# Expert weights in chunks of 128 rows by 1024 columns; light groups of two PSUM banks, heavy groups of four

## The chip, the cores and the metric

The kernel is one program on one core of a Trainium2 chip. The metric is the device time of one execution in microseconds (us), the median of several runs. The engines are TensorE (PE; its weight loads are shown apart as PEld), VectorE (DVE), ScalarE (ACT), GpSimd (POOL) and SyncE (SP), which issues nearly all DMAs. TensorE's clock has two levels, 1.2 and 2.4 GHz; the profile gives the granted clock as a share of the higher one.

## What is computed

Two layers of a diffusion backbone run over 256 latent and 256 context tokens with a width of 1024. Each layer is a modulated RMSNorm, a mixer (neighbourhood attention, differential attention, short convolution, output projection) and a feed-forward part. In the second layer that part is eight experts, of which each latent token takes two. This is the stage that the change touches:

```python
def swiglu(h, w1, w3, w2):
    return (jax.nn.silu(h @ w1) * (h @ w3)) @ w2

def moe_ffn(h, w_router, w1, w3, w2):
    logits = jnp.einsum('...d,de->...e', h.astype(jnp.float32), w_router.astype(jnp.float32))
    top_vals, top_idx = lax.top_k(logits, TOP_K)
    top_w = jax.nn.softmax(top_vals, axis=-1)
    gates = jnp.sum(jax.nn.one_hot(top_idx, N_EXPERTS, dtype=jnp.float32) * top_w[..., None], axis=-2).astype(h.dtype)
    y = jnp.zeros_like(h)
    for e in range(N_EXPERTS):
        y = y + gates[..., e:e + 1] * swiglu(h, w1[e], w3[e], w2[e])
    return y
```

`w1` and `w3` of an expert are 1024 x 3584, `w2` is 3584 x 1024, all float32. Here h has 256 tokens. The output is the RMSNorm of the latent stream after this.

## The kernel before

**Experts by rank.** The router's counts rank the experts. The program holds a branch for each pattern of counts; with these inputs the one that runs (`moe_main`) treats ranks 0 and 1 as heavy and ranks 7, 2, 3, 4, 5 as light, with room for 32 tokens each (64 for rank 2); one expert is not called on. A *heavy* expert multiplies all 256 tokens: every weight chunk is split into a high and a low part (`whi` by ACT, L467, and `wlo` by DVE, L469), and each product is three fast matmuls (L220 to L222): high by high, low by high, high by low. A *light* expert gathers its few tokens and makes plain float32 products (L1575) whose 32 tokens fill only 32 of PE's rows, so four products sit side by side; a *fold* (L1603) adds the four sums up and brings the columns into rows.

**Weights.** The 588 chunks of 512 KB of the seven experts stream in through a ring of 20 buffers (`raw`) and, at first, 16 more (`far`). A chunk is 256 rows by 512 columns, as two rows of 512 columns on each of 128 partitions (`load`, L1189); `weights` (L1343) hands out the next buffer of the ring and issues its DMA on SP's queue, which waits there until the buffer's last reader is done.

**Heavy experts.** `heavy` (L1504) goes through the 3584 hidden columns in groups of 3, 2 and 2 times 512. In a group it takes 512 columns at a time: four chunks of `w1` into two PSUM banks (of four, tag H), a Silu of both, four chunks of `w3` into the other two banks, then the product (DVE, L1539) and its split into `gh` and `gl`. Then come the group's rows of `w2`, first for the output's left half in two banks (two blocks of 128 tokens), then for the right half. After each half, `gated` (L1457, tile `of`) scales the two banks and `accumulate` (L1464) adds them to `xT`. `split_ahead` (L1356) asks for the split of one chunk more than is in use, so the split of the next chunk is written into ACT's and DVE's order at a point of its own. `heavy` yields after every chunk: 84 steps an expert.

**Light experts.** `light` (L1562) takes 512 columns of `w1` at a time, four chunks into one bank (of two, tag L), then the same of `w3`. At the end of each, ACT copies the bank to `s` (L1596), and the fold of it is run in the middle of a later group. `w2` is done for one half of the output after the other, and `scatter` (L1468) after each half scales it, splits it (`oh`, `ol`), and a later task multiplies by the selection matrix (L1482, L1483) and adds to `xT`. It yields after every two chunks: 42 steps an expert, two chunks or four products each.

**The order.** `mix_experts` (L1641) writes one program from both: a planner counts the estimated costs (`HEAVY` 2.85 for a heavy step, `PE_COST` for a light one) against the chunks loaded, and switches between heavy steps, one at a time, and bursts of two light steps (`BURST`). Matmuls are chained in exactly this order (`chained`, L1374). Before the branch, while routing is being finished, `first_steps` (L1328) already runs rank 7's first products from the 36 chunks that are loaded in advance.

```python
            elif burst == 0:
                k = "heavy" if surplus <= lead else "light"
                burst = BURST if k == "light" else 1
```

The rest of the functions that the change touches:

Of the kernel before, what the change touches and what calls it, by code (L numbers as in the profile page):

```python
# [23 lines left out]
KT = 8  # L24
# [5 lines left out]
RAW_M = 20  # L30
# [4 lines left out]
FAR = 16  # L35
ROT = 0
# [5 lines left out]
BURST = 2  # L42

# [84 lines left out]
def tile_hybrid_block(ctx: ExitStack, tc: tile.TileContext, x, c, cx, c_ctx, ada_w, ada_b, w_in, w_out, na_rpb,  # L128
# [1021 lines left out]
    def route_early():  # L1150
# [28 lines left out]
        mo["chunks7"], mo["early"] = heavy_chunks([7], (7,)), {}  # L1179
        ahead(mo["raw"])  # L1180

    def ahead(places):

        for raw in places:
            w, r, row0, c0 = next(mo["chunks7"])
            mo["early"][w.tensor.name, r, row0, c0] = raw
            load(w, slice(0, 1), row0, c0, raw)

    def load(w, e, row0, c0, raw):  # L1189
        sy.dma_start(out=raw, in_=w[0][e, row0:row0 + 256, c0:c0 + 512].rearrange("e (k p) n -> p (e k) n", p=128))  # L1190
# [6 lines left out]
    def route():  # L1197
# [7 lines left out]
        for n in ("h", "split", "hpool", "rawd"):  # L1205
# [4 lines left out]
            [128, 2, 512], F32, name=f"far{i}") for i in range(FAR)])  # L1210
# [117 lines left out]
    def first_steps():  # L1328

        run = mo["run7"] = light((7,), 32)  # L1330
        while mo["early"]:
            next(run)
            mo["run7_done"] = mo.get("run7_done", 0) + 1
        while mo["folds"]:
            mo["folds"].popleft()()
        mo["run7_tasks"] = list(tasks)
        tasks.clear()
        mo["far"].close()

# [3 lines left out]
    def weights(w, r, row0, c0):  # L1343

        raw = mo["early"].pop((w.tensor.name, r, row0, c0), None)
        if raw is None:
            raw = mo["ring"].popleft()
            if r < 7 and r not in mo["e"]:
                mo["e"][r] = nc.values_load(mo["ints"][0:1, 1, r:r + 1], engines=[mybir.EngineType.SP], min_val=0,
                                            max_val=NE - 1)  # L1350
            load(w, bass.ds(mo["e"][r], 1) if r < 7 else slice(0, 1), row0, c0, raw)
        if any(raw is q for q in mo["raw"]):
            mo["ring"].append(raw)
        return raw

    def split_ahead(chunks):  # L1356
# [3 lines left out]
        def make():  # L1360
            for args in chunks:
                raw = weights(*args)
                hi, lo = (mo["split"].tile([128, 2, 512], F32R, name=n, tag=n) for n in ("whi", "wlo"))
                parts(raw, hi, lo)
                yield hi, lo
        todo = make()
        ready.append(next(todo))
# [100 lines left out]
    def scatter(o, h, selT, gate, after):  # L1468

        big = mo["big"]  # L1470
        while mo["adds"]:
            mo["adds"].popleft()()
        of = gated(o, h, gate)
        oh = big.tile([128, 512], F32R, name="oh", tag="oh")
        ol = big.tile([128, 512], F32R, name="ol", tag="ol")
# [14 lines left out]
    def heavy_chunks(ranks, groups):  # L1490

        for r in ranks:
            j0 = 0
            for nj in groups:
                for j in range(j0, j0 + nj):
                    for w in (moe_w1, moe_w3):
                        for u in range(4):
                            yield w, r, u * 256, j * 512
                for h in range(2):
                    for q in range(2 * nj):  # L1500
                        yield moe_w2, r, j0 * 512 + q * 256, h * 512
                j0 += nj

    def heavy(last, ranks):  # L1504
# [3 lines left out]
        pieces = split_ahead(heavy_chunks(ranks, mo["groups"]))  # L1508
        for r in ranks:
            j0 = 0  # L1510
            for nj in mo["groups"]:
                gh, gl = (mo["gated"].tile([128, 4 * max(mo["groups"]), 256], F32R, name=n, tag=n)
                          for n in ("gh", "gl"))
                for j in range(nj):
                    sa = None
                    for w in range(2):
                        a = [pbank("H").rearrange("p (a b) -> p a b", a=2) for _ in range(2)]
                        for k in range(0, KT, 2):
                            wh, wl = next(pieces)
                            for kk in range(2):  # L1520
                                kt = k + kk
                                for f in range(4):
                                    fs = slice(f * 128, (f + 1) * 128)
                                    for q in mm3(a[f // 2][:, f % 2, :], wh[:, kk, fs], wl[:, kk, fs], xs[0][:, kt, :],
                                                 xs[1][:, kt, :], kt == 0 and f % 2 == 0, kt == KT - 1):
                                        chained(q)
                            if k < KT - 2:
                                yield
                        if sa is None:
                            sa = [xT[:, 4 * i:4 * i + 4, 384:512] for i in range(2)]  # L1530
                            a = [q.rearrange("p a (b c) -> p (a b) c", c=128) for q in a]
                            for i in range(2):
                                act.activation(sa[i], a[i], AF.Silu)
                        else:
                            for i in range(2):
                                f0 = 4 * j + 2 * i
                                q, gs = a[i].rearrange("p a (b c) -> p (a b) c", c=128), [
                                    v[:, f0:f0 + 2, :].rearrange("p a (b c) -> p (a b) c", c=128) for v in (gh, gl)]
                                dve.tensor_tensor(out=sa[i], in0=sa[i], in1=q, op=ALU.mult)  # L1539
                                parts(sa[i], *gs)  # L1540
                        yield
                j0 += nj
                for h in range(2):
                    o = [pbank("H") for _ in range(2)]
                    for f0 in range(0, 4 * nj, 2):
                        wh, wl = next(pieces)
                        for k in range(2):
                            f = f0 + k
                            for b in range(2):
                                bs = slice(b * 128, (b + 1) * 128)  # L1550
                                for q in mm3(o[b], gh[:, f, bs], gl[:, f, bs], wh[:, k, :], wl[:, k, :], f == 0,
                                             f == 4 * nj - 1):
                                    chained(q)
                        if f0 < 4 * nj - 2:
                            yield
                    for b in range(2):
                        accumulate(b, h, gated(o[b], h, mo["rk"][:, 2 + b, r:r + 1]))
                    if j0 == 7 and r == ranks[-1]:
                        last(h)
                    yield  # L1560

    def light(ranks, n, last=None):  # L1562
# [16 lines left out]
        for i, r in enumerate(ranks):  # L1579
# [4 lines left out]
            for j in range(7):  # L1584
                for w in (moe_w1, moe_w3):
                    a = pbank("L")
                    for u in range(4):
                        raw = weights(w, r, u * 256, j * 512)
                        for k in range(2):
                            product(a, x[:, 2 * u + k, i * n:(i + 1) * n], raw[:, k, :], 2 * u + k, KT)  # L1590
                        if u == 1:
                            yield
                    while folds:
                        folds.popleft()()
                    s = mo["pool"].tile([128, 512], F32, name="s", tag="s", bufs=2)
                    act.activation(s, a, AF.Copy)  # L1596

                    def fold(s=s, gs=g[j], first=w is moe_w1):

                        p = pbank("tg")[:, :4 * n].rearrange("p (a b) -> p a b", a=4)  # L1600
                        if n == 32:
                            for c in range(4):
                                chained(pe.matmul(p[32 * c:32 * c + 32], fold32,  # L1603
                                                  s.rearrange("p (q c i) -> p c q i", c=4, i=32)[:, c], start=True,
                                                  stop=True, tile_position=(0, 32 * c), skip_group_check=True))
                            t = mo["pool"].tile([128, 4, n], F32, name="sT", tag="sT", bufs=2)
                            dve.transpose(out=t, in_=p)  # L1607
                            p = t
                        else:
                            for f in range(4):  # L1610
                                chained(pe.matmul(p[:, f, :], s[:, f * 128:(f + 1) * 128], mo["fold", n], start=True,
                                                  stop=True))
                        if first:
                            act.activation(gs, p, AF.Silu)
                        else:
                            dve.tensor_tensor(out=gs, in0=gs, in1=p, op=ALU.mult)
                    folds.append(fold)
                    yield
                if j == 3:
                    tasks.append(place)  # L1620
            end = i == len(ranks) - 1
            if end:
                mo["following"]()
            for h in range(2):
                o = pbank("L")
                for q in range(14):
                    raw = weights(moe_w2, r, q * 256, h * 512)
# [211 lines left out]
```

## Time and profile before

| | us |
|---|---|
| median of 3 runs | 1720.82 |
| lowest, highest | 1720.62, 1724.28 |
| the profiled execution | 1725.1 |
| its span, first to last instruction | 1723.4 |
| PE busy | 1651.9 |
| DVE busy | 1022.4 |
| ACT busy | 633.3 |

The profile is of one execution: its own time is 1725.1 us, of which 1723.4 lie between the first and the last instruction. Busy times are of the whole span; the expert stage is the second half of it, from about 880 us on, and is read by windows. In a timeline row the bracket is the idle time before the instruction and what ended it. The mean granted clock of the span is 0.980.

### The profile page before, as it was taken

The page shows a single profiled execution, that of the slowest core. Times are in us where ns is not written, and L with a number is a line of the kernel's source. Part 1 is how long each engine was busy: PE and PEld are TensorE (multiplying, and loading weights), DVE is VectorE, ACT ScalarE, POOL GpSimd, SP SyncE. Part 2 cuts the span into 40 slices and gives each one's busy share as a digit, 9 for nine tenths or more (in the row PEclk, how much of TensorE's full clock was granted, in tenths as well). Part 3 has the DMA queues.
Part 4 walks back from the last instruction along what each step waited for, and adds up shares of the span by engine and source line. Part 5 has one row for each costly group of instructions (what it writes and reads, how often), then busy time and mean ns, then how long its engine had stood idle before and what let it go on. Part 6 is the DMA issues. An engine that isn't in the chain of part 4 may idle for free.

```text
span 1723.4 us, 28476 instructions
## 1 busy us (share of the span) xinstructions
PE 1651.9 (96%) x10942; PEld 1269.6 (74%) x10942; DVE 1022.4 (59%) x2027; ACT 633.3 (37%) x1057; POOL 17.4 (1%) x27
## 2 busy tenths in 40 slices
PE   7999999999999999999987999999999999999996
PEld 5787778988878888988763875566777787686873
DVE  4768977888877774788853432233444544544444
ACT  4555444422212222555443332222333333333332
POOL 0101000000000000000010000000000000000000
PEclk9999999999999999999888999999999999999998
DMA  9744243355555552342599999999999999999996
GB/s 286 179 128 108 98 147 98 99 175 192 195 172 171 174 201 78 109 125 74 200 342 363 387 378 349 345 330 351 372 370 365 343 380 357 383 358 352 376 364 214
DMA packets 302288, 434.65 MB, mean 252 GB/s; under 512 B 23496, under 2 KB 142784, under 8 KB 302144
## 3 DMA queue, kind: packets, MB, share of 16 engines
q1 hardware_dynamic: 300656, 432.14, 73.6%
q8 instruction: 87, 1.43, 0.3%
q10 hardware_dynamic: 1488, 0.62, 0.1%
q14 instruction: 57, 0.47, 0.1%
HBM read 431.66 MB, written 1.05 MB: 251 GB/s over the span
## 4 chain that ended last, share of the span: by engine, by line
PE 84%; DVE 7%; DMA 4%; ACT 2%; issue 1%; SPq 1%; DVEq 0%; ACTq 0%
PE L L1575 13%; PE H L220 10%; PE H L222 9%; PE H L221 9%; PE mm L220 8%; PE mm L222 8%; PE mm L221 8%; PE at L220 4%; PE at L221 4%; PE at L222 4%; DMA raw<-in_moe_w_dram 2%; DVE rope_t L480 1%; PE at L578 1%; PE at L561 1%; DVE wlo L469 1%
## 5 line engine op out<-in xcount | busy, mean ns | idle before, releaser
L469 DVE TENSOR_TENSOR wlo<-raw,whi 128x1024 fp32r<-128x1024 f32 x168 | 201.6, 1222 | 135.1 <-ACT whi L467 127.3
L222 PE MATMUL H<-xh,wlo 128*128 128x256 f32 x896 | 255.1, 285 | 9.4 <-DVE wlo L469 9.4
L220 PE MATMUL H<-xh,whi 128*128 128x256 f32 x896 | 259.4, 290 | 1.5 <-ACT whi L467 1.5
L221 PE MATMUL H<-xl,whi 128*128 128x256 f32 x896 | 254.0, 284 | 0.0
L220 PE MATMUL mm<-hh,whi 128*128 128x512 f32 (+1 forms) x648 | 231.6, 358 | 2.2 <-ACT hh L467 1.7
L221 PE MATMUL mm<-hl,whi 128*128 128x512 f32 (+1 forms) x648 | 226.6, 350 | 0.0
L222 PE MATMUL mm<-hh,wlo 128*128 128x512 f32 (+1 forms) x648 | 226.5, 351 | 0.0
L98 ACT ACTIVATE whi<-raw 128x1024 fp32r<-128x1024 f32 x130 | 134.4, 1056 | 237.1 <-DMA raw<-in_ffn_w_dram 144.8
L467 ACT ACTIVATE whi<-raw 128x1024 fp32r<-128x1024 f32 x168 | 171.2, 1049 | 61.7 <-PE H L221 25.6
L220 PEld LDWEIGHTS H<-xh,whi 128*128 128x128 f32 x896 | 172.2, 192 | 25.8 <-issue 17.0
L99 DVE TENSOR_TENSOR wlo<-raw,whi 128x1024 fp32r<-128x1024 f32 x130 | 157.0, 1221 | 56.1 <-ACT whi L98 55.4
L222 PEld LDWEIGHTS H<-xh,wlo 128*128 128x128 f32 x896 | 172.1, 192 | 11.5 <-DVE wlo L469 11.3
L221 PEld LDWEIGHTS H<-xl,whi 128*128 128x128 f32 x896 | 172.1, 192 | 0.5
L1596 ACT ACTIVATE s<-L 128x512 f32<-128x512 f32 x70 | 41.8, 597 | 297.1 <-PE L L1575 297.1
L220 PEld LDWEIGHTS mm<-hh,whi 128*128 128x128 f32 x648 | 123.8, 191 | 22.4 <-issue 4.0
L222 PEld LDWEIGHTS mm<-hh,wlo 128*128 128x128 f32 x648 | 123.5, 191 | 16.8 <-issue 2.1
L221 PEld LDWEIGHTS mm<-hl,whi 128*128 128x128 f32 x648 | 124.1, 192 | 13.8 <-issue 0.5
L1575 PE MATMUL L<-raw,xT 128*32 128x512 f32 (+1 forms) x896 | 133.2, 598 | 0.0
L320 DVE SCALAR_TENSOR_TENSOR ada_t<-raw,scol,ada_t 128x256 f32<-128x256 f32 x266 | 116.6, 481 | 2.8
L1607 DVE STREAM_TRANSPOSE sT<-tg 128x128 f32<-128x128 f32 x56 | 17.8, 317 | 163.0 <-PE tg L1603 162.7
L221 PE MATMUL H<-wlo,gh 128*128 128x512 f32 x224 | 88.9, 397 | 3.0 <-DVE wlo L469 3.0
L220 PE MATMUL H<-whi,gh 128*128 128x512 f32 x224 | 90.9, 406 | 0.0
(308 smaller groups left out, 2760.8 us busy)
## 6 DMA issues: line engine op xcount, KB each, us to landing
raw<-in_moe_w_dram SPq DMA_DIRECT2D x572, 512.0 KB, 7.4
raw<-in_ada_w_dram SPq DMA_DIRECT2D x40, 1024.0 KB, 5.2
raw<-in_ffn_w_dram SPq DMA_DIRECT2D x32, 1024.0 KB, 5.5
raw<-in_w_in_dram SPq DMA_DIRECT2D x12, 1024.0 KB, 5.2
raw<-in_w_in_dram SPq DMA_DIRECT2D x24, 512.0 KB, 5.3
aw<-in_ada_w_dram SPq DMA_DIRECT2D x16, 512.0 KB, 7.4
far<-in_moe_w_dram SPq DMA_DIRECT2D x16, 512.0 KB, 9.1
raw<-in_w_out_dram SPq DMA_DIRECT2D x5, 1024.0 KB, 5.6
```

Source lines behind the costliest of these rows:

```text
L98: self.nc.scalar.activation(hi, r, AF.Copy)
L99: self.nc.vector.tensor_tensor(out=lo, in0=r, in1=hi.bitcast(F32), op=ALU.subtract)
L220: return [pe.matmul(o, ah, bh, start=start, stop=False, **kw), pe.matmul(o, ah, bl, start=False, stop=False, **kw), pe.matmul(o, al, bh, s ...
L221: pe.matmul(o, ah, bl, start=False, stop=False, **kw),
L222: pe.matmul(o, al, bh, start=False, stop=stop, **kw)]
L320: dve.scalar_tensor_tensor(out=t[:, g, :], in0=raw[:, kt, :], scalar=scol[:, kt, g:g + 1], in1=t[:, g, :], op0=ALU.mult, op1=ALU.add)
L467: act.activation(hi, src, AF.Copy, scale=scale)
L469: dve.tensor_tensor(out=lo, in0=src, in1=hi.bitcast(F32), op=ALU.subtract)
L480: dve.tensor_tensor(out=t[32 * o:32 * o + 32, :], in0=src[32 * i:32 * i + 32, :], in1=sin_t[32 * i:32 * i + 32, :], op=ALU.mult)
L1575: chained(pe.matmul(o[c * n:(c + 1) * n, :], lhs, rhs, start=(k < ng), stop=(k >= nk - ng), tile_position=(0, c * n), skip_group_check=True))
L1596: act.activation(s, a, AF.Copy)
L1607: dve.transpose(out=t, in_=p)
```

## The change

A weight chunk becomes 128 rows by 1024 columns, one row of 1024 columns on each partition; `w2` comes in whole rows. The last 512 of the 3584 hidden columns of `w1` and `w3` keep the old form. All experts, heavy and light, go through the hidden columns in `GROUPS` of 2, 2, 2 and 1 times 512. Number and size of the DMAs are the same, 588 of 512 KB.

A light group fills both L banks (`quad`: four chunks, four products into the one bank and then four into the other), so a light step has eight products and there are 21 steps an expert, at twice the planner's cost. Both banks' copies and folds come together; `w2` fills one bank for each half of the output, and both halves are scattered at the end. A heavy group of `w1` or `w3` fills all four H banks. Its first six chunks go over the four banks each; the last two are taken together, and each bank gets its products of both before the next (`by_bank`); `heavy` yields once in between, after the second bank. `w2` does the same with two halves by two blocks of tokens, and accumulates all four banks after that. `first_steps` stops with four chunks left over (`TAIL`), which the mixed part takes first. Splits (`whi`, `wlo`) have three buffers as before.

```diff
+GROUPS = (2, 2, 2, 1)
...
+    def load(w, e, row0, c0, nk, raw):
+        sy.dma_start(out=wide(raw).rearrange("p (k n) -> p k n", k=nk),
+                     in_=w[0][e, row0:row0 + 128 * nk, c0:c0 + 1024 // nk].rearrange("e (k p) n -> p (e k) n", p=128))
...
+    def first_chunks_of(w, r, j0, nj):
+        for k in range(0, KT, 3 - nj):
+            yield w, r, k * 128, j0 * 512, 3 - nj
...
     def first_steps():
         run = mo["run7"] = light((7,), 32)
-        while mo["early"]:
+        while len(mo["early"]) > TAIL:
             next(run)
...
     def heavy(last, ranks):
+        def by_bank(n, products):
+            for k in range(n - 2):
+                piece = next(pieces)
+                for b in range(4):
+                    products(b, k, piece)
+                yield
+            two = [next(pieces) for _ in range(2)]
+            for b in range(4):
+                for i in range(2):
+                    products(b, n - 2 + i, two[i])
+                if b == 1:
+                    yield
...
+            for j0, nj in col_groups(GROUPS):
...
+                for w in range(2):
+                    a = [pbank("H").rearrange("p (a b) -> p a b", a=2) for _ in range(2 * nj)]
...
+                    if nj == 2:
+                        yield from by_bank(KT, products)
...
+                    for i in range(2 * nj):
+                        q = a[i].rearrange("p a (b c) -> p (a b) c", c=128)
+                        if w == 0:
+                            gate(sa[i], q)
                         else:
+                            up(sa[i], q, *(v[:, 2 * i:2 * i + 2, :].rearrange("p a (b c) -> p (a b) c", c=128)
+                                           for v in (gh, gl)))
+                    yield
+                o = [pbank("H") for _ in range(4)]
...
+                yield from by_bank(4 * nj, out_products)
+                for i in range(4):
+                    h, b = divmod(i, 2)
+                    accumulate(b, h, gated(o[i], h, mo["rk"][:, 2 + b, r:r + 1]))
...
     def light(ranks, n, last=None):
+            def quad(banks, lhs, u, nk, per):
+                raws = [weights(*next(chunks)) for _ in range(4)]
+                for h, bank_ in enumerate(banks):
+                    for k in range(4 * per):
+                        cs = (h if per == 1 else k % 2) * 512
+                        product(bank_, lhs(4 * per * u + k), raws[k // per][:, cs:cs + 512], 4 * per * u + k, nk)
...
+            for j0, nj in col_groups(GROUPS):
+                for w in range(2):
+                    a = [pbank("L") for _ in range(nj)]
+                    for u in range(nj):
+                        quad(a, latents, u, KT, 3 - nj)
+                        if u == 0 and not (nj == 1 and w):
+                            fold_all()
+                        if u < nj - 1:
                             yield
+                    for h in range(nj):
+                        folded(a[h], j0 + h, w == 0)
                     yield
...
+            o = [pbank("L") for _ in range(2)]
+            for u in range(7):
+                quad(o, columns, u, 28, 1)
...
             for h in range(2):
-                o = pbank("L")
...
+                scatter(o[h], h, *v["v"], last if end else None)
+            yield
...
-                    "light": deque((PE_COST[n][k >= 28], 1.0) for r, n in lights for _ in r for k in range(42))}
+                    "light": deque((2 * PE_COST[n][k >= 14], 2.0) for r, n in lights for _ in r for k in range(21))}
```

How the instructions move is shown at three places of the branch that runs. First PE, early in the mixed part, where rank 7's light products stand between heavy ones (`x` are the gathered tokens, `tg` the bank of a fold). Before:

```order
L222 MATMUL H<-xh,wlo 128x256
L1575 MATMUL L<-raw_8733,x_9166 32x512 x2
L1575 MATMUL L<-raw_8737,x_9166 32x512 x2
L1575 MATMUL L<-raw_8661,x_9166 32x512 x2
L1575 MATMUL L<-raw_8665,x_9166 32x512 x2
L1603 MATMUL tg<-s,fold_101 32x128 x4
L220 MATMUL H<-xh,whi 128x256
```

The change:

```order
L224 MATMUL H<-xh,wlo 128x256
L1619 MATMUL L<-raw_8717,x_9166 32x512 x2
L1619 MATMUL L<-raw_8721,x_9166 32x512 x2
L1619 MATMUL L<-raw_8725,x_9166 32x512 x2
L1619 MATMUL L<-raw_8729,x_9166 32x512 x2
L1640 MATMUL tg<-s,fold_101 32x128 x8
L1619 MATMUL L<-raw_8733,x_9166 32x512 x2
L1619 MATMUL L<-raw_8737,x_9166 32x512 x2
L1619 MATMUL L<-raw_8661,x_9166 32x512 x2
L1619 MATMUL L<-raw_8665,x_9166 32x512 x2
L222 MATMUL H<-xh,whi 128x256
```

A burst between two heavy matmuls had eight products and one fold; now it has sixteen products and the folds of two banks. In the whole branch the order has 86 such bursts between heavy runs before and 44 with the change; the products are the same in number.

Next DVE, at the end of a heavy `w2` group (`of` scales an output bank, `xT` takes the sum, `wlo` is the low part of a later chunk). Before:

```order
L1460 SCALAR_TENSOR_TENSOR of<-H,rk,gf 128x512
L469 TENSOR_TENSOR wlo<-raw_8709,whi 128x1024
L1466 TENSOR_TENSOR xT<-xT,of 128x4x128
L1460 SCALAR_TENSOR_TENSOR of<-H,rk,gf 128x512
L469 TENSOR_TENSOR wlo<-raw_8713,whi 128x1024
L1466 TENSOR_TENSOR xT<-xT,of 128x4x128
```

The change:

```order
L471 TENSOR_TENSOR wlo<-raw_8737,whi 128x1024
L471 TENSOR_TENSOR wlo<-raw_8661,whi 128x1024
L1491 SCALAR_TENSOR_TENSOR of<-H,rk,gf 128x512 x2
L1497 TENSOR_TENSOR xT<-xT,of 128x4x128 x2
L1491 SCALAR_TENSOR_TENSOR of<-H,rk,gf 128x512 x2
L1497 TENSOR_TENSOR xT<-xT,of 128x4x128 x2
L471 TENSOR_TENSOR wlo<-raw_8665,whi 128x1024
```

One bank's `of` stood ahead of the `wlo` of the next group's first chunk, and the other's `of` ahead of the second chunk's. Now the `wlo` of the next group's first chunk (the second row) stands ahead of all four banks, and the second chunk's (the last row) behind all four.

Last PE, a burst in which one light group ends and the next begins (each line is a product, L with a number a bank's use). The change:

```order
L1619 MATMUL L_58652<-raw13_8713,xT_64 32x512
L1619 MATMUL L_58652<-raw14_8717,xT_64 32x512
L1619 MATMUL L_58652<-raw15_8721,xT_64 32x512
L1619 MATMUL L_58652<-raw16_8725,xT_64 32x512
L1619 MATMUL L_58849<-raw17_8729,xT_64 32x512
L1619 MATMUL L_58849<-raw18_8733,xT_64 32x512
L1619 MATMUL L_58849<-raw19_8737,xT_64 32x512
L1619 MATMUL L_58849<-raw0_8661,xT_64 32x512
L1619 MATMUL L_58850<-raw17_8729,xT_64 32x512
```

The first four products are the last of the second bank of a group. The next group's first bank, which has the same place in PSUM as the group's first one, follows in the same burst, and then its second. The order has six such places in the mixed part with room for 32 tokens.

## Rows read from the trace of the kernel before

**Rows 1.** The page, sections 1 and 4.

```profile
PE 1651.9 (96%) x10942; PEld 1269.6 (74%) x10942; DVE 1022.4 (59%) x2027; ACT 633.3 (37%) x1057; POOL 17.4 (1%) x27
...
PE 84%; DVE 7%; DMA 4%; ACT 2%; issue 1%; SPq 1%; DVEq 0%; ACTq 0%
```

**Rows 2.** Windows: us, engines busy (instructions), PEclk, DMA share, GB/s.

```profile
1150.00:1700.00 550.00, 539.04 (x4051) 402.59 (x4049) 247.86 (x314) 189.06 (x248) 0.00 (x0) 1.00 1.01 363
sum 756.00, PE 742.36 PEld 539.47 DVE 312.25 ACT 246.40 POOL 0.00; mean PE 247.45 PEld 179.82 DVE 104.08 ACT 82.13 POOL 0.00
```

**Rows 3.** PE's waits, 940 to 1700: total us, times, longest.

```profile
PE H L222 <- DVE wlo L469: 9.4, 9, 1.7
PE H L221 <- DVE wlo L469: 3.0, 3, 1.1
PE tg L1482 <- ACT oh L467: 1.5, 2, 0.7
```

**Rows 4.** The DMA queue's waits, 940 to 1700, same columns.

```profile
SPq L1190 <- PE L L1575: 215.7, 189, 5.2
SPq L1190 <- DVE wlo L469: 197.0, 138, 4.7
```

**Rows 5.** DMA, 944 to 1016, expert weights.

```profile
DMA packets 14403, 27.83 MB, mean 387 GB/s; under 512 B 847, under 2 KB 847, under 8 KB 14398
```

**Rows 6.** DMA, 825 to 838 in 40 slices, `w_out` in its first half.

```profile
GB/s 0 0 0 139 25 151 429 391 416 416 416 429 416 429 353 391 441 416 429 416 290 25 38 13 38 0 0 0 0 113 50 101 258 378 416 397 403 403 410 378
```

**Rows 7.** Timeline, PE: start, us, line, operation, count, [idle before, releaser].

```profile
1243.11 0.39 PE L221 MATMUL H<-wlo,gh 128*128 128x512 f32 x1
1243.34 0.39 PE L222 MATMUL H<-whi,gl 128*128 128x512 f32 x1
1243.66 1.92 PE L1575 MATMUL L<-raw,xT 128*32 128x512 f32 x16
...
1245.73 0.50 PE L220 MATMUL H<-whi,gh 128*128 128x512 f32 x1
```

**Rows 8.** Timeline of the first light steps, PE and ACT.

```profile
910.82 1.89 PE L1575 MATMUL L<-far,x 128*32 128x512 f32 x16
...
912.75 1.46 PE L1575 MATMUL L<-far,x 128*32 128x512 f32 x12
912.84 0.60 ACT L1596 ACTIVATE s<-L 128x512 f32<-128x512 f32 x1 [1.11 <-PE L L1575]
```

**Rows 9.** Timeline of DVE, then PE, at a `w2` end.

```profile
1259.29 0.75 DVE L1460 SCALAR_TENSOR_TENSOR of<-H,rk,gf 128x512 f32<-128x512 f32 x1 [1.61 <-PE H L222]
1259.96 1.21 DVE L469 TENSOR_TENSOR wlo<-raw,whi 128x1024 fp32r<-128x1024 f32 x1
...
1261.22 0.39 PE L222 MATMUL H<-xh,wlo 128*128 128x256 f32 x1 [1.06 <-DVE wlo L469]
```

**Rows 10.** Groups, 880 to 1723: count, busy us, mean ns, idle before, releasers.

```profile
L469 DVE TENSOR_TENSOR wlo<-raw,whi 128x1024 fp32r<-128x1024 f32 x168 | 201.6, 1222 | 135.1 <-ACT whi L467 127.3 <-PE L L1575 6.0 <-DMA raw<-in_moe_w_dram 1.6
...
L467 ACT ACTIVATE whi<-raw 128x1024 fp32r<-128x1024 f32 x168 | 171.2, 1049 | 61.7 <-PE H L221 25.6 <-PE H L222 21.6 <-issue 12.2
...
L1460 DVE SCALAR_TENSOR_TENSOR of<-H,rk,gf 128x512 f32<-128x512 f32 x24 | 17.4, 750 | 31.0 <-PE H L222 31.0
...
L1466 DVE TENSOR_TENSOR xT<-xT,of 128x512 f32<-128x512 f32 x24 | 15.7, 684 | 0.0
```

**Rows 11.** Timeline of the end, PE and DVE.

```profile
1701.21 0.74 PE L1482 MATMUL tg<-oh,selT 128*128 128x512 f32 x2 [1.54 <-ACT oh L467]
...
1709.79 0.75 DVE L1460 SCALAR_TENSOR_TENSOR of<-L,gate,gf 128x512 f32<-128x512 f32 x1 [3.91 <-PE L L1575]
...
1711.30 0.69 DVE L469 TENSOR_TENSOR ol<-of,oh 128x512 fp32r<-128x512 f32 x1 [0.76 <-ACT oh L467]
```

**Rows 12.** Timeline of PE at the first heavy product.

```profile
938.76 0.38 PE L220 MATMUL H<-xh,whi 128*128 128x256 f32 x1 [1.54 <-ACT whi L467]
```

**Rows 13.** DMA queue, 880 to 1723: packets, MB, share of 16 engines.

```profile
q1 hardware_dynamic: 153768, 296.39, 97.8%
```

More of the change, by code (lines that the diff above doesn't have):

```diff
@@ L35 @@
 FAR = 16
+TAIL = (RAW_M + FAR) % 8
 ROT = 0
@@ L1362, in make @@
                 raw = weights(*args)
-                hi, lo = (mo["split"].tile([128, 2, 512], F32R, name=n, tag=n) for n in ("whi", "wlo"))
+                hi, lo = (mo["split"].tile([128, 1024], F32R, name=n, tag=n) for n in ("whi", "wlo"))
                 parts(raw, hi, lo)
@@ L1366, in split_ahead @@
         todo = make()
+        if mo["tight"]:
+            yield from todo
+            return
         ready.append(next(todo))
@@ L1488, in scatter, with heavy_chunks @@
         tasks.append(lambda: mo["adds"] and mo["adds"].popleft()())
-    def heavy_chunks(ranks, groups):
+    def heavy_chunks(ranks):
         for r in ranks:
[L1493 to L1502, printed above, removed]
+            for j0, nj in col_groups(GROUPS):
+                for w in (moe_w1, moe_w3):
+                    yield from first_chunks_of(w, r, j0, nj)
+                for f in range(4 * nj):
+                    yield moe_w2, r, (4 * j0 + f) * 128, 0, 1
@@ L1504, in heavy @@
     def heavy(last, ranks):
         xs = mo["x"]
-        pieces = split_ahead(heavy_chunks(ranks, mo["groups"]))
-        for r in ranks:
[L1510 to L1517, printed above, removed]
+        pieces = split_ahead(heavy_chunks(ranks))
@@ L1518, in heavy @@
                         for k in range(0, KT, 2):
-                            wh, wl = next(pieces)
+                            piece = next(pieces)
                             for kk in range(2):
-                                kt = k + kk
                                 for f in range(4):
[L1523 to L1526, printed above, removed]
+                                    use(k + kk, f, *(v[:, kk * 512 + f * 128:kk * 512 + (f + 1) * 128] for v in piece))
@@ L1583, in place @@
                 v["v"] = places(r, n)
[L1584 to L1591, printed above, removed]
-                            yield
[L1593 to L1617, printed above, removed]
@@ L1618, in light @@
                     yield
-                if j == 3:
+                if j0 == 2:
                     tasks.append(place)
@@ L1657, in mix_experts @@
         mo["xs"] = mo["hT"] if end else mo["big"].tile([128, KT, 128], F32, name="xs")
-        mo["ring"] = deque(mo["raw"])
-        mo["adds"], mo["groups"], mo["e"] = deque(), groups, {}
+        if begun:
+            mo["early"] = mo["left"]
+        mo["ring"] = deque(v for v in mo["raw"] if not any(v is q for q in mo["early"].values()))
+        mo["adds"], mo["e"] = deque(), {}
         left = [2 if heavies else 1]
@@ L1778, in moe_general @@
             with tc.If(n2 > 64) as many:
-                mix_experts([7, 0, 1, 2], [((r,), 128) for r in range(3, 6)], groups=(2, 2, 2, 1))
+                mix_experts([7, 0, 1, 2], [((r,), 128) for r in range(3, 6)])
             with many.Else():
@@ L1787, in moe_general @@
                 with tc.If(n0 > 128) as uneven:
-                    mix_experts([0, 1, 2], [((7,), 64)] + [((r,), 128) for r in range(3, 6)], groups=(2, 2, 2, 1))
+                    mix_experts([0, 1, 2], [((7,), 64)] + [((r,), 128) for r in range(3, 6)])
                 with uneven.Else():
```

160 lines of the change are left out of this document (96 added, 64 removed).

## The prediction

> **What bounds the kernel now.** The change touches only the experts, so I first ask what their stage, from about 940 us to the end, is limited by. The page gives PE 96% of the span and 84% of the chain that ended last, against 4% for DMA [rows 1]. An average can hide a stage with another limit, so next the windows: between 944 and 1700 us the matmuls are busy 742.4 of 756 us; in the longest stretch, from 1150 us on, at a granted clock of 1.00, while the DMA share is 1.01 too [rows 2]. Two resources look full. The waits tell which one sets the pace: PE's waits sum to 13.9 us in these 760 us, 12.4 on DVE's `wlo` and 1.5 on ACT's `oh`, and none on a DMA [rows 3]. The DMA queue, in contrast, waits for PE and DVE to give ring buffers back: 215.7 us for light matmuls and 197.0 us for `wlo` alone [rows 4]. So transfers are held back by consumption: they ran at 387 GB/s while the ring filled [rows 5], and at 363 GB/s later [rows 2]. A share near 1 here means that something is always outstanding, not that PE lacks data. **PE is the bound, with some 14 us of waits on top.** The matmuls themselves (numbers, sizes, products) stay; only switches between their forms and waits can move.
>
> **The sum, part by part.** It is made against the profiled execution, 1725.1 us (span 1723.4, 1.7 us around it); the median of the runs is 1720.8, 4.3 lower. A difference under 0.2% (3.4 us) cannot be told from no change.
>
> *Rows of 1024 columns.* The number of transfers and their bytes stay; a descriptor grows from 2 to 4 KB. I cost it at nothing: PE never waits for these transfers, and the ring's release paces them. That cover would be gone only if PE outran the ring, and then the bound is rival G below. Below nothing there is no reason to go: the wider rows in this trace did not run slower (about 416 GB/s for `w_out` in 4 KB rows [rows 6] beside 387 [rows 5]).
>
> *Fewer switches.* Going from a heavy to a light matmul costs 0.09 us: the next start is 0.32 after the last heavy one (1243.34 to 1243.66) where heavy ones follow each other at 0.23. The burst with its fold takes 2.07 us until H starts again (1243.66 to 1245.73) [rows 7]; the same burst followed by light work takes 1.93 (910.82 to 912.75) [rows 8]. So the way back costs 0.14, or 0.09 if there is no fold at the end; a pair costs 0.18 to 0.23. The order has 86 such bursts between heavy runs before, 44 after: 42 × 0.18 = **−7.6**; bounds −3.8 (half of it reappears as fold switches inside a burst) and −9.2.
>
> *The `wlo` waits.* At the end of a heavy `w2` group, DVE's order puts `of` of the first bank ahead of the next piece's `wlo`: `of` waited 1.61 us for the matmuls, `wlo` started at 1259.96 and PE stood 1.06 us for it at 1261.22 [rows 9]. Twelve such waits are the 12.4 us [rows 3]. In the new order the first next piece's `wlo` stands ahead of all of a group's `of` and `xT`, at all seven ends: **−12.4**. But the second next piece's `wlo` now stands behind four `of` and four `xT`: 4 × 750 + 4 × 684 = 5.7 us of DVE [rows 10]. The first two need banks ended earlier. An estimate by durations: a bank's last two pieces are 6 matmuls at 0.23, so banks end 1.37 us apart; the block then holds DVE until 2.3 us after the last bank, and `wlo` (1222 ns) ends at 3.5. PE needs it after one piece of 24 matmuls at 0.117 to 0.13, about 3.0. So 0.5 us at the two ends that go straight on to heavy pieces, and 2.2 at one where a scatter's DVE work joins it; light bursts cover the other four: **+3.3**; bounds 0 and +12.4 (the same waits again).
>
> *Two banks per light group.* There are two L banks and one group takes both. Where a burst ends one group and begins the next, the first product of the new group must wait until ACT has copied that bank: the copy began 0.13 us after PE's end and takes 0.60, and PE has the other bank's four products in between, half of the 1.89 of eight, 0.95 [rows 8]. So an idle ACT is just in time; one that is inside a `whi` (1049 ns [rows 10]) is late by half of it on average. The order has six such places with n=32 in the heavy stretch and three in the first steps, where nothing is split: 6 × 0.5 = **+3**; bounds 0 and 9 × 1.05 = 9.5.
>
> *Expert ends.* Both halves' results are now scattered at once, so one more `of` and `ol` (0.75 + 0.69 us [rows 11]) stand in DVE's queue at each of four inner ends. Tasks are given out one or two a step, with matmuls between: I take **+2**, between 0 and 4 × 1.44 = 5.8.
>
> *Start of the heavy part.* PE waited 1.54 us for the first `whi` [rows 12]; on ACT it now stands behind two `s` copies (0.60 each [rows 8]) instead of one, and the `wlo` after it is as late: I take **+1**, bounds 0 and +2. Eight products of the first steps move behind the branch; they cost the same there.
>
> *The tail.* After the last product today one half's `of`, `oh`, `ol`, `tg` and two `xT` remain; then there are two halves'. One more `of`, `ol` and pair of `xT` (as long as the 684 ns of [rows 10]) on DVE is 0.75 + 0.69 + 1.37 = 2.8, with the starts between them 3.0. The wait of the first half's `tg` at 1701.21 (1.54) [rows 11] goes: **+1.5**, bounds 0 and +4.
>
> Sum: −7.6 − 12.4 + 3.3 + 3 + 2 + 1 + 1.5 = **−9.2**. The profiled execution goes to 1715.9, the median to 1711.6. With every bound at its best it is −9.2 − 12.4 = −21.6 (1699); with every bound at its worst −3.8 − 12.4 + 12.4 + 9.5 + 5.8 + 2 + 4 = +17.5 (1738).
>
> The trace's waits at group ends (1.06 us at 1261.22) come from an evacuation that stands before the next group's split. The Trainium skill, Perfetto Trace Analysis, section Optimizing Tensor Performance, says that independent matmul groups should rotate through different PSUM banks so that evacuating one overlaps the matmuls of the next. The change gives a group all the banks there are; by this rule the time is that of rival S.
>
> **The rivals.**
>
> *S, slower: no spare bank.* Before, a heavy group used two of four H banks, so the next group started in the other two while DVE and ACT emptied the first. After it, the next group's bank 0 is the bank just ended. Ending the last two pieces bank by bank is meant to hide this: bank 0 is ended 3 × 1.37 us before bank 3. But DVE must give 1.4 us per bank at a `w2` end (750 + 684 ns [rows 10]), and at a `w3` end as much, just what PE takes for a bank's last pieces, and each `wlo` (1222 ns) that stands among them makes it one bank late. Two heavy experts with four groups have 16 `w3` and `w2` ends; with DVE late by one bank each costs about 1.9 us (the 1.4 of a bank on top of the 0.5 found above), 30 us instead of the 3.3 counted: −9.2 − 3.3 + 30 = +17.5, **about 1738**. It decides from an average wait of 0.8 us per end on (12.5 / 16), where the gain is gone. For it: the ends are where PE waits already [rows 3, 9], and DVE's block grows from one of/xT pair to four. Against it: DVE is busy only 248 of 550 us [rows 2], and bank ends are spread over 4.1 us.
>
> *N, no change.* The new waits and the longer tail pay back all of the 20 us: waits of 0.8 us on average at the sixteen ends do it, or the upper bounds of the `L` banks and the expert ends. A part of this case is that the freed 12.4 us come back elsewhere, since DVE does the same work and only its order differs. 1717.4 to 1724.2, **about 1721**.
>
> *G, large gain: DMA sets the end after all.* Then 2 KB rows are the limit: 90% of the 296.4 MB [rows 13] go from 387 to 416 GB/s [rows 5, 6], which at the present total is 296.4 / 0.387 = 766 us against 718 (0.9 × 296.4 / 0.416 + 0.1 × 296.4 / 0.387): −48, **about 1673**. Against it: no wait of PE on a transfer in 760 us [rows 3], and 400 us of the queue's waits are for consumers [rows 4]. The Trainium skill, Perfetto Trace Analysis, section DMA Optimizations, advises descriptors larger than 2 KB where a kernel is DMA-bound; the trace agrees that 4 KB rows ran faster, but not that this kernel is so bound.
>
> *The change does not do what it says* for PE, since bursts may be cut differently: the order shows 44 against 86 bursts, so only the price per burst is open.
>
> **How the numbers follow.** The forecast (a gain of 3.4 to about 21 us) gets 0.46: its main terms are read from order and rows. G 0.07. N 0.22. S 0.25: DVE has room on average, but the blocks at ends are worked out by hand to about 1 us each. Faster is 0.46 + 0.07. The forecast's own range is 1699 to 1717; the range that leaves out G and the upper half of S goes from 1698 to 1735.
>
> **What would show it.** Right: PE's waits on `wlo` fall from 12.4 to a few us; new waits of `L` on ACT's `s` at some six places, each 0.3 to 1; transfers still not among PE's waits, and the DMA queue still waiting for PE and DVE at 340 to 390 GB/s; bursts with 0.09 and 0.14 at their edges; some 3 us more between the last `L` product and the first `sm`. Wrong for the better: PE's busy time itself falls, or an idle that the waits do not list. Wrong for the worse (S): waits of `H` on `gh`, `gl`, `sa` or `of`, over 0.8 us on average at sixteen ends, or a granted clock below 1.00 in the windows of the heavy part.

## The result and the profile after

The changed kernel takes 1709.3 us (median of 20 runs, 1705.2 to 1722.3) against 1721.5 (20 runs, 1717.5 to 1728.4): a ratio of 0.9937, interval 0.9926 to 0.9947, or some 11 us (the two medians lie 12.2 apart). Forecast were 1711.6 and a range of 1698 to 1735. The two profiled executions differ by more, 1725.1 to 1709.1, because that of before lies 3.6 us over its median.

Engines and windows of the changed kernel, the page's first section and the windows of [rows 2]:

```profile
PE 1639.5 (96%) x10942; PEld 1265.7 (74%) x10942; DVE 1030.1 (60%) x2043; ACT 639.0 (37%) x1057; POOL 17.6 (1%) x27
```

```profile
1150.00:1700.00 550.00, 536.04 (x4031) 398.83 (x4029) 262.37 (x345) 196.54 (x256) 0.00 (x0) 1.00 0.95 365
sum 756.00, PE 741.95 PEld 543.63 DVE 327.99 ACT 256.15 POOL 0.00; mean PE 247.32 PEld 181.21 DVE 109.33 ACT 85.38 POOL 0.00
```

PE is as full as before. The DMA share has fallen from 1.01 to 0.95, in part because the changed kernel's loads end within this window: up to 1690 us it is 0.97. PE's waits from 940 to 1690 (engine, line, releaser: total us, times, longest), the counterpart of [rows 3]:

```profile
PE H L222 <- ACT gh L469: 3.1, 2, 1.6
PE H L224 <- DVE gl L471: 1.2, 2, 0.6
PE H L224 <- DVE wlo L471: 1.1, 1, 1.1
PE H L223 <- DVE wlo L471: 0.9, 2, 0.8
PE H L222 <- ACT whi L469: 0.8, 1, 0.8
PE H L222 <- DVE of L1491: 0.8, 1, 0.8
```

13.9 us have become 7.9, and they are other ones: `wlo` has fallen from 12.4 to 2.0, `tg` on `oh` from 1.5 to nothing, and 5.9 us on `gh`, `gl`, `whi` and `of` are new. No wait of `L` on ACT's `s` is among them, and none on a DMA. The DMA queue still waits for the readers of the ring (counterpart of [rows 4]), and while the ring fills it moves 401 GB/s where it moved 387 [rows 5]:

```profile
SPq L1194 <- PE L L1619: 176.2, 111, 9.8
SPq L1194 <- DVE wlo L471: 145.9, 91, 6.1
```

```profile
DMA packets 7915, 28.88 MB, mean 401 GB/s; under 512 B 882, under 2 KB 882, under 8 KB 7909
```

The largest new wait is at the last group of a heavy expert, whose 512 columns use two banks that end together. ACT and PE there (timeline):

```profile
1329.27 1.06 ACT L469 ACTIVATE whi<-raw 128x1024 fp32r<-128x1024 f32 x1 [1.82 <-PE H L223]
1330.23 1.14 ACT L469 ACTIVATE gh<-xT 128x512 fp32r<-128x512 f32 x2
...
1330.90 0.50 PE L222 MATMUL H<-whi,gh 128*128 128x512 f32 x1 [1.55 <-ACT gh L469]
1331.23 0.40 PE L223 MATMUL H<-wlo,gh 128*128 128x512 f32 x1
1332.24 0.50 PE L224 MATMUL H<-whi,gl 128*128 128x512 f32 x1 [0.61 <-DVE gl L471]
```

`w2` follows `w3` at once, and the `whi` of a later chunk stands ahead of `gh` on ACT.

**An account that closes.** To see all of the time and not only what the waits list, I took the starts of PE's matmuls from the first light product to the last matmul, and took from each interval the usual one of its kind (0.12 us after a heavy matmul of 256 columns, 0.23 after one of 512, and so on). All kernels here have the same matmuls, so the usual part is the same and the excess, sorted by what lies on both sides, tells where they differ. In us, with the time after the last matmul:

```
                                before  after    e1     e4     e9    e11
usual intervals                  739.1  738.5  738.7  739.1  738.6  738.5
heavy to light burst               7.7    3.9    3.9    7.9    3.9    3.9
first interval after a burst       8.9    4.6    4.5    8.8    4.5    4.5
light burst to heavy              18.0   12.7    9.0   18.0    9.0    9.0
joints inside bursts               0.4    2.8    6.3   -0.4    3.6    4.2
heavy waits over 0.3              14.4   10.5    9.9   18.4    8.2    3.2
heavy, 0.05 to 0.3                 3.8    5.1    1.8    7.8    3.1    0.5
to, in and from tg of oh, places  12.4   10.0   18.4   11.4   18.0   18.9
wait behind the branch             8.4    8.6    8.4    8.3    8.2    8.3
first heavy product                1.8    2.3    1.8    1.8    1.8    1.8
after the last matmul             11.0   11.9   11.0   11.0   11.0   11.0
sum                              825.8  811.0  813.6  832.1  809.9  803.8
```

Of the 14.8 us between the two profiles, the four rows on bursts hold 10.9 (35.0 to 24.1) and the two on heavy intervals 2.6. e1 to e11 are the experiments below. Each column is one execution. The trace of e12, a second one of the changed kernel, has a sum of 812.5; it agrees within 0.1 us in the heavy rows and at the edges of the bursts, and differs in the light products at the start of the stage, where the granted clock is below 1 (0.84 and 0.80 in the windows 890 to 915 and 915 to 940). Of the changed kernel's 8.6 behind the branch, 7.3 are the wait itself.

### The profile page after: what moved, and what is told of

The parts are those of the page before. It is cut to its first block, busy times and chain, and to the rows that moved or that the text cites. A ratio compares the mean times of both kernels' runs of the same rounds, so it can differ in the third digit from the quotient of the medians.

```text
span 1707.3 us, 28490 instructions
## 1 busy us (share of the span) xinstructions
PE 1639.5 (96%) x10942; PEld 1265.7 (74%) x10942; DVE 1030.1 (60%) x2043; ACT 639.0 (37%) x1057; POOL 17.6 (1%) x27
## 5 line engine op out<-in xcount | busy, mean ns | idle before, releaser
L1619 PE MATMUL L<-raw,xT 128*32 128x512 f32 (+1 forms) x896 | 137.2, 597 | 0.3
L223 PEld LDWEIGHTS mm<-hl,whi 128*128 128x128 f32 x648 | 123.3, 190 | 13.7 <-issue 0.5
```

The source lines that it names most:

```text
L223: pe.matmul(o, ah, bl, start=False, stop=False, **kw),
L1619: chained(pe.matmul(o[c * n:(c + 1) * n, :], lhs, rhs, start=(k < ng), stop=(k >= nk - ng), tile_position=(0, c * n), skip_group_check=True))
```

## The experiments

Each ran beside the kernel before, e1 to e4 on one chip, e5 to e8 on a second, e9 to e12 on a third; a ratio is to the kernel before on the same chip, with its 95% interval. The theory was mine: the gain is fewer switches and fewer end waits, the row width gives nothing.

**e1: only longer bursts.** The kernel before, with one number changed:

```diff
-BURST = 2
+BURST = 4
```

> The kernel before with bursts of four light steps (16 products) in place of two: 44 bursts between heavy runs instead of 86, chunks and banks as before. Theory (the gain is fewer switches and fewer end waits, the row width is worth nothing): 42 fewer pairs of entry and exit at 0.18 to 0.23 us, 7.6 to 9.7 us less, ratio 0.9945 to 0.9956; the waits for wlo stay near 12 us. Rival (the wider rows bring the gain): 1.000, since the rows stay at 2 KB.

0.9930 (0.9909 to 0.9950): the whole gain, with the old chunks, banks and heavy code, and more than the switches' own price by the sum. The rival on rows falls. By the account the burst rows give 11.3 us and the heavy rows 6.6, while 6.0 are lost again at the `tg` products of the scatter, which now split light bursts. The waits for `wlo` did not stay near 12 us, as expected; by the list they fell to 7.6:

```profile
PE H L222 <- DVE wlo L469: 5.6, 6, 1.1
PE H L221 <- DVE wlo L469: 2.0, 2, 1.1
```

So longer light bursts shorten waits of heavy products too, with two banks as before. A burst of it on PE (timeline: start, us, line, operation, count):

```profile
1255.92 1.92 PE L1575 MATMUL L<-raw,xT 128*32 128x512 f32 x16
1257.66 0.40 PE L1603 MATMUL tg<-s,fold 128*32 128x128 f32 x8
1257.88 1.90 PE L1575 MATMUL L<-raw,xT 128*32 128x512 f32 x16
1259.60 0.40 PE L1603 MATMUL tg<-s,fold 128*32 128x128 f32 x8
1259.93 0.39 PE L220 MATMUL H<-xh,whi 128*128 128x256 f32 x1
1260.15 0.28 PE L221 MATMUL H<-xl,whi 128*128 128x256 f32 x1
1260.27 0.28 PE L222 MATMUL H<-xh,wlo 128*128 128x256 f32 x1
```

From light to heavy it takes 4.01 us, where two bursts of 2.07 [rows 7] take 4.14. And the first heavy interval is 0.22 (1259.93 to 1260.15), the next one 0.12: a price of 0.10 that the forecast had not seen. It stands in the kernel before too, right behind the heavy matmul at 1245.73, the last of [rows 7]:

```profile
1246.06 0.39 PE L221 MATMUL H<-wlo,gh 128*128 128x512 f32 x1
1246.29 0.40 PE L222 MATMUL H<-whi,gl 128*128 128x512 f32 x1
```

0.33, then 0.23.

**e2: the changed kernel with bursts of one step** (`BURST = 1`), 8 products.

> The changed kernel with bursts of one light step (8 products): 86 bursts again. Theory: 7.6 to 9.7 us above the changed kernel, ratio to before 0.998 to 0.9995, and the entries 0.09 us each in the trace. Rival (rows): as the changed kernel, 0.9937.

0.9945 (0.9926 to 0.9965): 1.4 us above the changed kernel's ratio, not 8. The burst rows of the account do rise as expected, from 24.1 to 32.1. But heavy waits over 0.3 fall from 10.5 to 8.2 (those of 0.05 to 0.3 rise from 5.1 to 6.9) and the `tg` row from 10.0 to 6.2. The waits from 940 to 1690:

```profile
PE H L224 <- DVE wlo L471: 2.7, 5, 0.9
PE H L222 <- ACT whi L469: 1.7, 2, 0.8
PE H L223 <- DVE wlo L471: 1.4, 2, 1.0
```

Those on `gh`, `gl` and `of` are gone. In the order, `w2` follows `w3` with no burst between at 2 places in place of 5, and scatter or place products follow light ones at 5 in place of 14. The expected sum per burst was right and the expectation for the whole wrong: the waits depend on where the bursts fall. It also means that longer bursts are not needed for the gain: with as many bursts as the kernel before, the changed kernel keeps 0.9945. Against the kernel before, its account has 2.9 us less at bursts, 3.1 less between heavy products and 6.2 less at `tg`. Which part of the new forms brings this was not tried.

**e3: light experts as changed, heavy ones as before** (two banks, 512 columns, groups of 2, 2, 2, 1).

```diff
-        pieces = split_ahead(heavy_chunks(ranks))
+        pieces = (tuple(v.rearrange("p (a b) -> p a b", b=512) for v in piece)
+                  for piece in split_ahead(heavy_chunks(ranks, mo["groups"])))
...
-    def mix_experts(heavies, lights, end=True, begun=False):
+    def mix_experts(heavies, lights, groups=(2, 2, 2, 1), end=True, begun=False):
```

> Light experts as changed (1024 columns, two banks, 16 products a burst), heavy experts as before in 512-column chunks and two banks, but in groups of 2, 2, 2, 1, which memory asks for. Theory: the switches' 8 us less and the waits for wlo as before or a little more (two more w2 ends): ratio 0.995 to 0.997, wlo waits 12 to 17 us. Rival (four banks bring the gain): 1.000 or over.

0.9911 (0.9886 to 0.9936), below the theory's 0.995 to 0.997 and at the changed kernel or under it (the intervals overlap). The waits for `wlo` came out at 3 us in place of 12 to 17. e8 below has the same heavy form with the old light bursts, and 13.6; so the new light form or its longer bursts take them away. Which of the two was not tried apart.

**e4: heavy experts as changed, light ones as before.** `light`, `scatter` and the order of the early chunks come from the kernel before, `TAIL = 0`.

> Heavy experts as changed (four banks, 1024 columns), light experts as before. Theory: 86 bursts stay, only the end waits change, from 14 to about 8 us: 4 to 7 us less, ratio 0.996 to 0.998. Rival (switches are all of the gain): 1.000. Rival (no spare bank): over 1.002.

1.0066 (1.0043 to 1.0088): slower, on the side of the rival that the forecast had called S. PE's waits from 940 to 1700:

```profile
PE H L222 <- ACT whi L469: 5.0, 7, 0.9
PE H L224 <- DVE wlo L471: 3.8, 5, 0.8
PE H L223 <- DVE wlo L471: 3.4, 4, 1.1
PE H L222 <- ACT gh L469: 1.6, 1, 1.6
```

They are on splits (12.2 us), not on banks. One place, ACT, DVE and PE:

```profile
1107.72 0.60 ACT L1641 ACTIVATE s<-L 128x512 f32<-128x512 f32 x1 [6.01 <-PE L L1620]
1108.66 0.38 ACT L1659 ACTIVATE g<-tg 128x256 f32<-128x256 f32 x1 [0.34 <-PE tg L1656]
1108.94 2.00 ACT L469 ACTIVATE whi<-raw 128x1024 fp32r<-128x1024 f32 x2
...
1110.02 2.36 DVE L471 TENSOR_TENSOR wlo<-raw,whi 128x1024 fp32r<-128x1024 f32 x2 [7.06 <-ACT whi L469]
...
1108.43 0.36 PE L222 MATMUL H<-xh,whi 128*128 128x256 f32 x1
...
1110.04 0.39 PE L222 MATMUL H<-xh,whi 128*128 128x256 f32 x1 [0.66 <-ACT whi L469]
...
1111.30 0.39 PE L224 MATMUL H<-xh,wlo 128*128 128x256 f32 x1 [0.76 <-DVE wlo L471]
```

PE comes back from a burst at 1108.43, makes six matmuls (bank 0's products of one chunk) and needs the next chunk at once: this is the step that takes the last two chunks together. One split was ready. The second stands on ACT behind the burst's `s` and `g`, which wait for PE, though ACT had been idle for 6.01 us before. A chunk that went over all four banks would have given 24 matmuls, 2.9 us, of cover. Waits of this form (three to eight matmuls after a burst) come to 14.2 us here, 2.0 in the changed kernel and none in e6, which has no such step. That the step is the cause is read from these places: e4 without it was not run.

**e5: rows of 2 KB again.** The halves of a buffer lie 16 bytes apart:

```diff
-        mo["raw"] = [stack(tc.tile_pool(name=f"rawm{i}", bufs=1)).tile([128, 2, 512], F32, name=f"raw{i}")
+        mo["raw"] = [stack(tc.tile_pool(name=f"rawm{i}", bufs=1)).tile([128, 2, 516], F32, name=f"raw{i}")
...
+        sy.dma_start(out=raw[:, :, :512], in_=w[0][e, row0:row0 + 128 * nk, c0:c0 + 1024 // nk].rearrange(
+            "e (k p) (a b) -> p (e k a) b", p=128, b=512))
```

> The changed kernel with the two halves of each buffer 16 bytes apart, so that every row of 1024 columns is written as two of 512 (2 KB) again; bytes, order, banks and DMA count stay. Theory: rows are worth nothing, ratio 0.9937 as the changed kernel within 0.001, while the filling stretch falls from 401 to about 387 GB/s. Rival (rows bring the gain): 0.998 or over.

0.9944 (0.9921 to 0.9966), and the filling stretch is back at 388 GB/s with twice the packets:

```profile
DMA packets 14458, 27.97 MB, mean 388 GB/s; under 512 B 845, under 2 KB 845, under 8 KB 14451
```

The wider rows make the transfers 3% faster and the kernel no faster that could be measured. The Trainium skill, Perfetto Trace Analysis, section DMA Optimizations, advises batching small transfers into larger ones, for example 2 KB into 4 or 8 KB, above all where a kernel is DMA-bound, and speaks of a dramatic gain in throughput. The runs agree on the direction and show 3%; this kernel is not so bound.

**e6: banks not ended one by one.**

```diff
-            for k in range(n - 2):
+            for k in range(n):
...
-                yield
-            two = [next(pieces) for _ in range(2)]
-            for b in range(4):
-                for i in range(2):
-                    products(b, n - 2 + i, two[i])
-                if b == 1:
-                    yield
+                if k < n - 1:
+                    yield
```

> The changed kernel with the last two chunks of a four-bank group going over all four banks like the others, so that the banks end within one chunk. Theory: ending bank by bank hides the evacuation; without it the direct ends between heavy groups wait for DVE and ACT, some nine of eighteen ends by 1 to 2.5 us: 9 to 22 us above the changed kernel, ratio 0.999 to 1.007. Rival (light bursts cover the ends anyway): 0.9937.

0.9979 (0.9966 to 0.9992), 7 us above the changed kernel: a little under the 9 to 22 expected. The waits:

```profile
PE H L224 <- DVE wlo L471: 3.6, 4, 1.2
PE H L222 <- ACT gh L469: 3.1, 2, 1.6
PE H L222 <- DVE of L1491: 2.7, 4, 0.8
PE H L223 <- DVE wlo L471: 1.4, 2, 1.2
PE H L224 <- DVE gl L471: 1.4, 3, 0.6
```

`of` and `wlo` take more, and the heavy rows of the account rise from 15.6 to 23.6. So with four banks a group, ending them one by one pays.

**e7: the changed kernel with a burst after each heavy `w3` and `w2` end.** `heavy` yields "edge" there, and the planner reads it:

```diff
+            if now == "edge" and "light" in runs:
+                k, burst = "light", BURST
```

> The changed kernel with one more rule in the planner: after the end of a heavy w3 or w2 group a light burst comes next. The trace of the changed kernel has four places with 9.2 us of waits at direct ends. Theory: these waits go, 7 to 9 us less, ratio 0.988 to 0.990. Rival (the bursts missing elsewhere make new waits, at ends of w1 or for the ring): 0.993 to 0.995.

0.9899 (0.9877 to 0.9920), within the theory's range. Heavy waits over 0.3 fall from 10.5 to 3.3; the `tg` row takes back 6.3.

**e8: the kernel before with groups of 2, 2, 2, 1.**

> The kernel before with heavy groups of 2, 2, 2, 1 times 512 columns in place of 3, 2, 2: two more w2 ends, nothing else. Theory: each w2 half's end costs one or two waits of about 1.1 us for wlo, so 2 to 5 us more, ratio 1.001 to 1.003. Rival (the number of ends does not matter): 1.000.

1.0031 (1.0018 to 1.0043): 5 us more, at the upper end of the range. The reason is only in part the expected one: the waits for `wlo` are 13.6 us where they were 12.4, and 2.5 us are new on `gh` and `gl`, at a `w3` end that `w2` follows at once. The change goes through the same groups; whether they cost it as much with four banks was not tried.

**e9: e4 with long bursts** (`BURST = 4`), the fourth corner of a table of two by two.

> Heavy experts as changed, light experts as before, bursts of four light steps (16 products): 44 bursts. With the heavy-only kernel (8 products a burst, 1.0066) and the kernel before with 16 (0.9930) this fills a table of two by two. Theory now (four banks emptied at an end need a burst of 4 us as cover, 2 us are too short): the waits of H fall from 16 to 8 us or less and the switches give 11 us, ratio 0.991 to 0.996. Rival (the four banks cost about 11 us whatever the bursts): 0.998 to 1.001.

0.9921 (0.9906 to 0.9936). The number is as the theory said, but e4's trace does not show the reason it gave: the waits there are on the second split, not on emptying banks. Fewer bursts meet the two-chunk step less often (4.7 us of such waits). With the old light form:

```
                        bursts of 8 products     of 16
heavy as before                1.0000           0.9930
heavy as changed               1.0066           0.9921
```

With the old light form, the heavy form costs 11 us with short bursts and nothing that can be told from zero with long ones. With the new light form short bursts do not cost this: the two entries of the lower row are then 0.9945 (e2) and 0.9937, and the waits at the two-chunk step come to 6.6 us in e2 against 14.2 in e4, with 86 bursts in both. Why the light form matters so much there is open.

**e10 and e11: the same rule at the ends as e7,** in the light-only kernel and in the kernel before with bursts of 16 products.

> The light-only kernel with a light burst after every heavy w3 and w2 end. Theory: its waits at ends (some 9 us) fall to 3 or less, given back in part by waits of tg on oh: ratio 0.985 to 0.990. Rival (the bursts are only moved, the waits go with them): 0.991.

> The kernel before with bursts of 16 products and a light burst after every heavy w3 and w2 end: no change of chunks or banks. Theory: its waits for wlo at ends (8 us) go, ratio 0.987 to 0.990, as fast as the changed kernel with the same rule. Rival (two-bank light groups and wide rows are needed): 0.993.

0.9878 (0.9862 to 0.9893) and 0.9888 (0.9872 to 0.9904): both beat both kernels. e11 needs no new chunks and no new banks, only another burst length and the rule. Its waits:

```profile
PE tg L1482 <- ACT oh L467: 6.4, 6, 1.9
PE H L222 <- DVE wlo L469: 1.9, 2, 1.0
PE tg L1483 <- DVE ol L469: 0.4, 2, 0.2
```

Heavy products hardly wait any more; what is left is the scatter's `tg`, whose place in light bursts costs 18.9 us in the account against 12.4 before.

**e12: the changed kernel again,** on the chip of e9 to e11.

> The changed kernel itself on the chip of the other three: 0.9937 as before, between 0.9926 and 0.9947. Other values would say that the chips differ by more than the kernels.

0.9938 (0.9922 to 0.9954). The interval of e10 lies below it altogether, and that of e11 too.

## Why the prediction was right, and where its steps were not

The bound was right: PE sets the pace before and after, no wait on a DMA appears in either list of waits from 940 us on, and rival G falls with e5, which gives the row width no effect. The sum of −9.2 came out at −11, and part of that closeness is luck, since its errors offset each other. In the account, whose two profiles lie 14.8 apart, the switches bring 3.3 us more than summed, the heavy waits 6.5 less, and the four terms of a loss, +7.5 together, come to about −0.5.

- *Fewer switches,* −7.6: mis-sized. The four rows on bursts say −10.9, or 0.26 us for each of 42 bursts, and −11.3 in e1. The step saw the entry (0.09) and the way out (0.14) and took 0.18; it had not looked one matmul further, where the first heavy interval is 0.10 longer.
- *The `wlo` waits,* −12.4 and +3.3: mis-sized. (The +3.3 is 3.2 by its own terms, two ends of 0.5 and one of 2.2.) `wlo` did fall by 10.4, and a `w2` end with a scatter does wait (1538 us, 2.2 in the account, the size that was worked out, but 1.0 of it is a wait for a bank behind `of`). But 5 us of the new waits are where no term was: on `gh` and `gl` at the last group's `w3` end (1329 and 1661, 2.5 each in the account), and 2.0 more at the two-chunk step (1198). By the list of waits heavy products got 4.5 us in place of the 9.1 forecast, by the account 2.6.
- *Two banks per light group,* +3: nothing of it appears. The other bank's four products, 0.95 us, were cover enough for a copy of 0.73, and no wait of `L` on `s` is in the list.
- *Expert ends,* +2: the two waits on `oh` went instead, −1.5. *Start,* +1: +0.5 in the account. *Tail,* +1.5: after the last `L` product the end takes 15.7 us where it took 13.7, and the wait of 1.54 before it is gone: +0.5.

Rival S, no spare bank, did not decide, but half of it is true: the heavy form alone, with the old light form and short bursts, is slower (e4), by a mechanism that it did not name, two splits wanted at once. The Trainium skill, Perfetto Trace Analysis, section Optimizing Tensor Performance, has groups rotate through banks so that one is emptied beside the next one's matmuls. The runs agree in so far as four banks that end together cost 7 us (e6), and ending them in turn does without a spare one when the bursts are long (e9). The largest thing the forecast got wrong is whose gain it is. It put 9.1 us to the heavy part. e1 shows that longer light bursts alone bring as much as the whole change, and e3 that the light part does without the four banks. Longer bursts are enough, but by e2 they are not the only way to the gain.

## What to carry to other kernels

Before reshaping data or banks to get longer runs of one kind of work, change the number that sets the run's length, and try that alone. Where two streams share an engine, put the switch where the one has just ended a group: the other's burst then covers the evacuation (e7, e10, e11). A step that uses two prepared operands at once needs two prepared, or the second one stands behind whatever was emitted between.

## What the runs showed that I had not expected

- Behind light products, folds and a placing's products, the interval from the first heavy matmul to the next is longer by some 0.10 us: 0.33 for 0.23 and 0.22 for 0.12, with a median excess of 0.10 in every kernel measured here. It is as long behind a wait (0.33 from 1330.90 to 1331.23), which the lists of waits do not count. Behind the scatter's `tg` products there is no excess (median 0.00 over 89 places).
- Rows of 4 KB moved 401 GB/s where those of 2 KB moved 387 (before, e1) and 388 (e5), all from 944 to 1016 us, while the ring fills.
- The `tg` products of scatters and places cost more where they split a light burst: the kernels with the old light form spend 18 to 19 us around them with long bursts (e1, e9, e11) and 11 to 12 with short ones.
